# Reads of partial sums moved behind the next stage's remainders, and seven block products for eight in the last quarter of an MLP

## The chip, the cores and the metric

The kernel runs on one core of one Trainium2 chip. The metric is device time in microseconds (us), the median of several runs; before the change it is 2062.33 us over three runs (2061.94 to 2062.93). One more execution was taken with the hardware profiler.

## The reference

One layer of a hybrid encoder over 256 tokens of width 2048: RMSNorm and two token mixers (chunked retention and gated delta rule) with one output projection, cross-attention into 256 memory tokens, a squared-ReLU MLP with hidden width 8192, and a final RMSNorm. All in float32. The change is in the MLP and in the final norm behind it:

```python
h = rms_norm(x, norm_ffn_g[l])
x = x + jnp.square(jax.nn.relu(h @ w_ff1[l])) @ w_ff2[l]
return rms_norm(x, norm_final_g)
```

## The kernel before

**Products in halves.** Every float32 operand is split into two `fp32r` halves: ACT rounds it (`whi`, line 125 for weights), DVE subtracts the rounded half and keeps the remainder (`wlo`, line 126). A product of two split operands is three matmuls: high by high, high by low, low by high. Weights come in loads of 1 MB into one of three tiles `raw`, issued on the queue of SyncE (SP); each is split in two halves of 1024 columns, into three pairs `whi`/`wlo`, and in the MLP every fourth time into a further pair `whx`/`wlx`. So at most four half stages of weights are split ahead of the matmuls.

**The MLP.** It runs in four quarters `fb` of 2048 hidden features. In each quarter first come eight calls of `blocks`, which make the quarter's hidden activations, transposed (lines 209 and 210), square them (`evac_h`) and split them into `hid`. Then they are multiplied with the quarter's 2048 rows of `w_ff2`, and the sums, scaled per token, are added to `res` (256 tokens by 2048 columns) by `add` (line 1138, a DVE instruction that reads PSUM). There are four blocks of 512 columns, n = 0 to 3, and four groups of 512 hidden features, q = 0 to 3.

**Seven for eight.** In the first three quarters `with_seven` does this second half. The part with q = 0, 1 and n = 0, 1 is seen as a product of two by two blocks (two halves of the tokens, even and odd groups of 128 features, two blocks of columns) and is computed as seven block products for eight, in the manner of Strassen and Winograd. It needs sums and differences of the activations (`token_sums`, called in `evac_h`, result `s_hl`) and of four weight blocks `b11`, `b12`, `b22` and `b21`, which `load_block` reads into the two large tiles `rt` and `tr`. A block is in two halves of 1024 columns. The stages, in the order of the matmuls, are `plain(n, q)` (24 matmuls of 128 x 512) and `product` (12 matmuls):

1. plain(3,0)  2. plain(3,1)  3. product of b11 into `shared`  4. plain(3,2)  5. product of b12-b11 into `p5`  6. plain(0,2)  7. product of b22 into own[1][0]  8. plain(3,3)  9. product of b22-b11 into `shared`, where b11 now holds the earlier difference  10. plain(0,3)  11. product of b21  12. plain(2,0)  13. product of b22-b12 into `shared`  14. plain(1,2)  15. plain(2,1)  16. product of b21-b11  17. plain(2,2)  18. plain(2,3)  19. plain(1,3).

`form` splits a block for a product: for stages 5, 9, 13 and 16 it first makes the difference in place on DVE (line 1188), half by half, then rounds (1190) and takes the remainder (1191). `triple` (line 1168) issues the matmuls, each held behind the last matmul of the stage before. After stages 3, 5, 8, 9, 11, 13, 16, 18 and 19 stand the `add` calls that read the finished sums.

**The last quarter** does the second half with `chunk` for each n (lines 166 to 168): 96 matmuls of 128 x 512 per block of columns. `evac_o` adds the sums, takes the sum of squares on ACT (`square_sum`, line 283) and multiplies with the final gain (1274). The last chunk is split more finely, holds the weights of q = 2, 3 in the tiles of the finished activations (`hold`), and its `evac_last` does the final norm and the stores. The gain is loaded into `b11` (`gfin`, line 1267) while the quarter's hidden activations are made.

**Order.** A planner writes each engine's order ahead of the run, from its own estimates of time. Instructions under `high_priority` come earlier when they are ready: fetches, roundings and remainders have offset 100000, `add` has 50000. `issue_after(x)` puts the instructions in it behind x on the same engine. On the chip every engine goes through its order as written.

Of the kernel before, what the change touches and what calls it, by code (L numbers as in the profile page):

```python
# [52 lines left out]
def trunk(ctx: ExitStack, tc: tile.TileContext, x_f, mem_f, positions, lead_f, small_f, w_in, ret_gn_g, w_out, w_xq,  # L53
# [1075 lines left out]
    ssq4 = cp.tile([P, NT, 5], F32, name="ssq4")  # L1129
    s_hl = tuple(fp.tile([P, 4, 512], F32R, name="s" + e, tag="s" + e, bufs=1) for e in "hl")  # L1130
    b11, b12, b22, b21 = (a[:, c:c + 8, :].rearrange("p k s -> p (k s)") for a in (rt, tr) for c in (0, 8))
    gfin = b11
    spare.append(fp)

    def add(n, t, ps, c0=0, c1=512):
        got = res[:, t, n * 512 + c0:n * 512 + c1]
        with tc.high_priority(offset=50000):
            vec.scalar_tensor_tensor(got, ps, rstd3q[:, t:t + 1], got, op0=ALU.mult, op1=ALU.add)
        return got

    def token_sums(i, hs):

# [8 lines left out]
    def with_seven(hid, rows):  # L1151
# [5 lines left out]
        opened, ends = set(), []  # L1157

        def load_block(to, which, n):

            src = rows[0:D // 2, n * 512:(n + 1) * 512].rearrange("(i two p) n -> p i two n", two=2, p=P)[:, :, which, :]
            with tc.issue_after(fetched[-1]), tc.high_priority(offset=100000):
                fetched.append(nc.sync.dma_start(to.rearrange("p (i n) -> p i n", i=4), src).ins)

        def triple(o, lhs, rhs, key, last=False):
            for j, (l, r) in enumerate(((0, 0), (0, 1), (1, 0))):
                with tc.issue_after(ends[-1]) if ends else ExitStack():
                    ins = pe.matmul(o, lhs[l], rhs[r], start=key not in opened, stop=last and j == 2,  # L1168
                                    skip_group_check=True).ins
                opened.add(key)  # L1170
            return ins

        def plain(n, q):
            halves = fetch(cols(rows, n * 512)(q), 4, 512)
            for i in range(4):
                for t in range(NT):
                    ins = triple(own[n][t], [a[:, i, t * P:(t + 1) * P] for a in hid[q]],
                                 [a[:, i % 2, :] for a in halves[i // 2]], (n, t), q == 3 and i == 3)
            ends.append(ins)

        def form(raw, minus=None):
            got = []
            with tc.high_priority(offset=100000):
                for c in range(2):
                    cs = slice(c * 1024, (c + 1) * 1024)
                    if minus:
                        with tc.issue_after(latest["lo"]):
                            vec.tensor_sub(raw[:, cs], *(a[:, cs] for a in minus))
                    hi, lo = (h[:, :1024] for h in half_tiles())
                    latest["hi"] = act.activation(hi, raw[:, cs], AF.Copy).ins  # L1190
                    latest["lo"] = vec.tensor_sub(lo, raw[:, cs], hi.bitcast(F32)).ins
                    got.append((hi.rearrange("p (k n) -> p k n", n=512), lo.rearrange("p (k n) -> p k n", n=512)))
            return got

        def product(o, lhs, halves, key):
# [10 lines left out]
        plain(3, 0)  # L1206
        load_block(b11, 0, 0)
        plain(3, 1)
# [9 lines left out]
        product(own[1][0], summed(3), form(b22), (1, 0))  # L1218
        plain(3, 3)
        load_block(b21, 1, 0)  # L1220
        for t in range(NT):
            add(3, t, own[3][t])
        product(shared, summed(1), form(b11, (b22, b11)), "shared")
        add(1, 0, shared)
        plain(0, 3)
        product(own[0][0], part(1, 0), form(b21), (0, 0))
        add(0, 0, own[0][0])
        plain(2, 0)
        product(shared, summed(2), form(b12, (b22, b12)), "shared")
        add(0, 1, shared)  # L1230
        add(1, 1, shared)
        plain(1, 2)
        plain(2, 1)
        product(own[0][1], part(1, 1), form(b11, (b21, b11)), (0, 1))
        add(0, 1, own[0][1])
        plain(2, 2)
        plain(2, 3)
        for t in range(NT):
            add(2, t, own[2][t])
        plain(1, 3)  # L1240
        for t in range(NT):
            add(1, t, own[1][t])

    for fb in range(4):
        hid = []
        rows = w_ff2[0, fb * D:(fb + 1) * D, :]
        for b2 in range(8):
            hs = fp.tile([P, 2, S], F32, name="hs", tag="hs", bufs=2)
            if b2 % 2 == 0:
                hid.append(quad_a())  # L1250

            def evac_h(b, ps):
                vec.scalar_tensor_tensor(hs[:, b, :], ps, 0.0, ps, op0=ALU.max, op1=ALU.mult)
                qh, ql = (a[:, b2 % 2 * 2 + b, :] for a in hid[-1])
                act.activation(qh, hs[:, b, :], AF.Copy)
                vec.tensor_sub(ql, hs[:, b, :], qh.bitcast(F32))
                if fb < 3 and b2 < 4 and b:
                    token_sums(b2, hs)

            blocks(h3, w_ff1[0], fb * D + b2 * 256, 2, evac_h)  # L1260
            if fb == 0:
                place(b2)
        if fb < 3:
            with_seven(hid, rows)
            continue
        with tc.issue_after(fetched[-1]):
            nc.sync.dma_start(gfin, norm_final_g.partition_broadcast(P))
        for n in range(4):
            ns = slice(n * 512, (n + 1) * 512)

            def evac_o(t, ps, c0, c1):
                got = add(n, t, ps)
                square_sum(ssq4[:, t, n:n + 1], got)
                vec.tensor_mul(got, got, gfin[:, ns])

            def evac_last(t, ps, c0, c1):
                got = add(n, t, ps, c0, c1)
                acc = ssq4[:, t, 4 if c0 else 3:5 if c0 else 4]
                if t == 0:
                    square_sum(acc, got)  # L1280
                else:
                    junk = sm.tile([P, 512], F32, name="junk", tag="junk", bufs=1)
                    vec.scalar_tensor_tensor(junk[:, :256], got, 1.0, got, op0=ALU.mult, op1=ALU.mult, accum_out=acc)
                if not c0:
                    s = sm.tile([P, 1], F32, name="s4", tag="s4")
                    vec.tensor_reduce(s, ssq4[:, t, 0:4], axis=AX.X, op=ALU.add)
                    vec.tensor_scalar(s, s, 1.0 / D, EPS, op0=ALU.mult, op1=ALU.add)
                    sums.append(s)
                else:
                    vec.scalar_tensor_tensor(sums[t], acc, 1.0 / D, sums[t], op0=ALU.mult, op1=ALU.add)  # L1290
                if c1 < 512:
                    return
                r = sm.tile([P, 1], F32, name="r4", tag="r4")
                rsqrt(r, sums[t])
                if t == 0:
                    vec.tensor_mul(res[:, t, ns], res[:, t, ns], gfin[:, ns])
                for c in (0, 3, 1, 2):
                    cs = slice(c * 512, (c + 1) * 512)
# [12 lines left out]


_INS = ["positions", "w_in", "ret_gn_g", "w_out", "w_xq", "w_xkv", "w_xo", "w_ff1", "w_ff2", "norm_final_g"]
# [39 lines left out]
```

## Time and profile before

| | us |
|---|---|
| median of three runs | 2062.33 |
| profiled execution | 2061.57 |
| its span, first to last instruction | 2059.9 |
| PE busy | 2047.6 |
| DVE busy | 1487.2 |
| ACT busy | 1119.7 |
| second halves of the first three quarters | 85.46, 85.79, 85.41 |
| first three blocks of columns, last quarter | 65.31 |

The granted TensorE clock is 0.999 of full speed over the span. PE is matmul, PEld the weight load of a matmul (which overlaps it), DVE VectorE, ACT ScalarE, SP the queue that issues most loads. A group of instructions is given as line, engine, operation, output<-inputs, shapes, count | busy us, mean ns | idle time of the engine just before, with what ended it. A row of a timeline is start, length, engine, line, operation, tiles, count and, in brackets, idle time before it with its releaser. The chain is the work that ended last, followed back from the last instruction.

### The profile page before, as it was taken

How to read it: one execution, taken by the hardware profiler on the slowest of the kernel's cores; microseconds unless marked ns; L12 is line 12 of the kernel's file. 1: busy time of each engine (PE TensorE's matmuls, PEld its weight loads, DVE VectorE, ACT ScalarE, POOL GpSimd, SP SyncE). 2: the span in 40 equal slices, each digit the busy share in tenths (PEclk: the TensorE clock that was granted, in tenths of full speed). 3: DMA queues.
4: the chain of work that ended last, by engine and by line, in shares of the span. 5: the costliest groups of instructions: out<-in, count | busy, mean ns of one | idle time of the engine just before them, and what ended most of it. 6: DMA issues, size and time to landing. Idle time of an engine off the chain costs nothing.

```text
span 2059.9 us, 28433 instructions
## 1 busy us (share of the span) xinstructions
PE 2047.6 (99%) x10886; PEld 1761.5 (86%) x10886; DVE 1487.2 (72%) x2369; ACT 1119.7 (54%) x1817; POOL 36.4 (2%) x50
## 2 busy tenths in 40 slices
PE   9999999999999999999999999999999999999998
PEld 7888888988888888888888898888888888888887
DVE  5887788779667975888567665777777777686654
ACT  5665764575457454755455555555445445444443
POOL 0000000000000000000000000000000000000000
PEclk9999999999999999999999999999999999999999
DMA  9679556455555555555467654679556646746653
GB/s 326 204 248 308 182 186 200 152 195 195 176 177 185 191 182 173 180 189 177 170 214 241 187 184 144 195 173 292 169 179 196 227 163 187 262 134 193 205 197 130
DMA packets 329225, 405.24 MB, mean 197 GB/s; under 512 B 34928, under 2 KB 239360, under 8 KB 328960
## 3 DMA queue, kind: packets, MB, share of 16 engines
q1 hardware_dynamic: 328656, 402.74, 61.0%
q8 instruction: 85, 1.39, 0.3%
q10 hardware_dynamic: 432, 0.69, 0.1%
q14 instruction: 52, 0.43, 0.1%
HBM read 389.74 MB, written 11.55 MB: 195 GB/s over the span
## 4 chain that ended last, share of the span: by engine, by line
PE 98%; DVE 1%; issue 0%; ACT 0%; DMA 0%; SPq 0%; POOLq 0%; POOL 0%; ACTq 0%
PE s L209 34%; PE s L210 18%; PE s L167 9%; PE s L166 9%; PE s L168 9%; PE b L1168 7%; PE s L1168 4%; PE s L398 1%; PE s L400 1%; PE s L399 1%; PE b L793 1%; PE b L696 1%; PE b L826 1%; PE b L138 0%; PE b L137 0%; PE b L139 0%
## 5 line engine op out<-in xcount | busy, mean ns | idle before, releaser
L126 DVE TENSOR_TENSOR wlo<-raw,whi 128x1024 fp32r<-128x1024 f32 x613 | 748.8, 1222 | 354.6 <-ACT whi L125 348.1
L209 PE MATMUL s<-q,whi 128*128 128x512 f32 x2816 | 974.1, 391 | 0.8 <-DVE bo L218 0.6
L125 ACT ACTIVATE whi<-raw 128x1024 fp32r<-128x1024 f32 x613 | 649.2, 1060 | 556.8 <-PE s L209 211.3
L210 PE MATMUL s<-q,wlo 128*128 128x256 f32 x2816 | 771.7, 281 | 0.0
L209 PEld LDWEIGHTS s<-q,whi 128*128 128x128 f32 x2816 | 521.1, 188 | 104.3 <-DVE bo L218 0.9
L210 PEld LDWEIGHTS s<-q,wlo 128*128 128x128 f32 x2816 | 528.7, 188 | 11.1 <-DVE wlo L126 0.8
L167 PE MATMUL s<-wlo,q 128*128 128x512 f32 x788 | 309.7, 393 | 0.0
L168 PE MATMUL s<-whi,q 128*128 128x512 f32 x788 | 307.3, 390 | 0.0
L166 PE MATMUL s<-whi,q 128*128 128x512 f32 x788 | 286.7, 390 | 0.0
L166 PEld LDWEIGHTS s<-whi,q 128*128 128x128 f32 x788 | 147.8, 188 | 30.9
L168 PEld LDWEIGHTS s<-whi,q 128*128 128x128 f32 x788 | 148.1, 188 | 29.7
L167 PEld LDWEIGHTS s<-wlo,q 128*128 128x128 f32 x788 | 148.1, 188 | 29.5
L217 ACT ACTIVATE bo<-s 128x256 f32<-128x256 f32 x192 | 72.9, 380 | 107.4 <-PE s L210 107.3
L218 DVE TENSOR_TENSOR bo<-bo,s 128x256 f32<-128x256 f32 x192 | 80.0, 417 | 53.6 <-ACT bo L217 53.3
L126 DVE TENSOR_TENSOR wlx<-raw,whx 128x1024 fp32r<-128x1024 f32 x59 | 72.2, 1223 | 37.2 <-ACT whx L125 36.3
L1168 PE MATMUL b<-whi,q 128*128 128x512 f32 x300 | 95.7, 389 | 0.0
L209 PE MATMUL s<-q,whx 128*128 128x512 f32 x256 | 89.7, 390 | 0.0
L125 ACT ACTIVATE whx<-raw 128x1024 fp32r<-128x1024 f32 x59 | 62.4, 1058 | 49.5 <-PE s L209 23.0
L210 PE MATMUL s<-q,wlx 128*128 128x256 f32 x256 | 71.3, 280 | 0.0
L655 DVE SCALAR_TENSOR_TENSOR acc<-bo,small,acc 128x255 f32<-128x255 f32 (+1 forms) x144 | 65.2, 479 | 1.8 <-ACT acc L652 0.6
L1168 PEld LDWEIGHTS b<-whi,q 128*128 128x128 f32 x300 | 56.3, 188 | 11.8
L1168 PE MATMUL b<-wlo,q 128*128 128x512 f32 x150 | 58.4, 389 | 0.0
(383 smaller groups left out, 2083.1 us busy)
## 6 DMA issues: line engine op xcount, KB each, us to landing
raw<-w_in SPq DMA_DIRECT2D x143, 1024.0 KB
raw<-w_ff SPq DMA_DIRECT2D x116, 1024.0 KB
raw<-w_xkv SPq DMA_DIRECT2D x29, 1024.0 KB
raw<-w_out SPq DMA_DIRECT2D x16, 1024.0 KB
raw<-w_xq SPq DMA_DIRECT2D x16, 1024.0 KB
raw<-w_xo SPq DMA_DIRECT2D x16, 1024.0 KB
rt<-w_ff SPq DMA_DIRECT2D x6, 1024.0 KB
tr<-w_ff SPq DMA_DIRECT2D x6, 1024.0 KB
```

The costliest lines, as they stand in the source:

```text
L125: latest["hi"] = act.activation(hi[:, cs], src[:, cs], AF.Copy).ins
L126: latest["lo"] = vec.tensor_sub(lo[:, cs], src[:, cs], hi[:, cs].bitcast(F32)).ins
L166: pe.matmul(o, xh, wh, start=first, stop=False)
L167: pe.matmul(o, xh, wl, start=False, stop=False)
L168: pe.matmul(o, xl, wh, start=False, stop=last)
L209: pe.matmul(ps[b], lh, xhl, start=kk == 0, stop=False)
L210: pe.matmul(ps[b][:, :S], ll, xh, start=False, stop=kk == KT - 1)
L217: act.activation(o, ps[b][:, S:], AF.Copy)
L218: vec.tensor_add(o, o, ps[b][:, :S])
L398: pe.matmul(o, xh, wh, start=kk == 0 and c0 == 0, stop=False)
L655: vec.scalar_tensor_tensor(acc[:, d:], ps[:, :S - d], cw[:, j, blk:blk + 1], acc[:, d:], op0=ALU.mult, op1=ALU.add)
L1168: ins = pe.matmul(o, lhs[l], rhs[r], start=key not in opened, stop=last and j == 2, skip_group_check=True).ins
```

## The change

- `add_later` puts an `add` behind the last remainder that has been written when it is called. `read` collects the sums to be read; `read_now` issues them, in the next stage, after that stage's roundings and remainders.
- `form` is gone. `product` splits its block and then, if told so (`then`), makes the difference that a later stage needs: b12-b11 at the end of stage 3, b22-b11 at that of 5, b22-b12 at that of 7, b21-b11 at that of 9.
- plain(1,2) comes before the product of b22-b12 (stages 13 and 14 change places).
- The last quarter uses `with_seven` too, with `last`: block of columns 2 takes the place of 3 in the interleaving, its four plain stages come in the places of plain(3,0) to plain(3,3), and the four plain stages of block 2 further on are left out. Block 3 remains as the finely split last chunk. `token_sums` runs in the last quarter as well.
- The final gain goes into `b22`, and its load stands behind the last fetch of `with_seven`. The square sums and the multiplications with the gain for blocks 0 to 2 come after `with_seven`, the multiplications behind the last `add`.

```diff
-    gfin = b11
+    gfin = b22
...
-            vec.scalar_tensor_tensor(got, ps, rstd3q[:, t:t + 1], got, op0=ALU.mult, op1=ALU.add)
+            latest["add"] = vec.scalar_tensor_tensor(got, ps, rstd3q[:, t:t + 1], got, op0=ALU.mult, op1=ALU.add).ins
         return got
+
+    def add_later(n, t, ps):
+
+        with tc.issue_after(latest["lo"]):
+            add(n, t, ps)
...
+        def read(*those):
+
+            reads.extend(those)
+
+        def read_now():
+            for those in reads:
+                add_later(*those)
+            reads.clear()
...
         def plain(n, q):
             halves = fetch(cols(rows, n * 512)(q), 4, 512)
+            read_now()
...
-        def form(raw, minus=None):
-            got = []
+        def product(o, lhs, raw, key, then=None):
+
+            halves = []
             with tc.high_priority(offset=100000):
-                for c in range(2):
-                    cs = slice(c * 1024, (c + 1) * 1024)
-                    if minus:
-                        with tc.issue_after(latest["lo"]):
-                            vec.tensor_sub(raw[:, cs], *(a[:, cs] for a in minus))
+                for c in range(0, 2048, 1024):
                     hi, lo = (h[:, :1024] for h in half_tiles())
-                    latest["hi"] = act.activation(hi, raw[:, cs], AF.Copy).ins
-                    latest["lo"] = vec.tensor_sub(lo, raw[:, cs], hi.bitcast(F32)).ins
...
+                    latest["hi"] = act.activation(hi, raw[:, c:c + 1024], AF.Copy).ins
+                    latest["lo"] = vec.tensor_sub(lo, raw[:, c:c + 1024], hi.bitcast(F32)).ins
+                    halves.append([a.rearrange("p (k n) -> p k n", n=512) for a in (hi, lo)])
+                for c in range(0, 2048, 1024) if then else ():
+                    with tc.issue_after(latest["lo"]):
+                        vec.tensor_sub(*(a[:, c:c + 1024] for a in then))
+            read_now()
...
+        first = 2 if last else 3
+        plain(first, 0)
         load_block(b11, 0, 0)
+        plain(first, 1)
         load_block(b12, 0, 1)
-        product(shared, part(0, 0), form(b11), "shared")
-        add(0, 0, shared)
-        plain(3, 2)
+        product(shared, part(0, 0), b11, "shared", (b11, b12, b11))
+        read((0, 0, shared))
+        plain(first, 2)
         load_block(b22, 1, 1)
-        product(p5, summed(0), form(b11, (b12, b11)), "p5")
-        add(1, 0, p5)
-        add(1, 1, p5)
+        product(p5, summed(0), b11, "p5", (b11, b22, b11))
+        read((1, 0, p5), (1, 1, p5))
         plain(0, 2)
...
+        product(own[1][0], summed(3), b22, (1, 0), (b12, b22, b12))
+        plain(first, 3)
         load_block(b21, 1, 0)
+        read(*((first, t, own[first][t]) for t in range(NT)))
+        product(shared, summed(1), b11, "shared", (b11, b21, b11))
+        read((1, 0, shared))
         plain(0, 3)
...
+        product(own[0][0], part(1, 0), b21, (0, 0))
+        read((0, 0, own[0][0]))
+        if not last:
+            plain(2, 0)
         plain(1, 2)
...
+        product(shared, summed(2), b12, "shared")
+        read((0, 1, shared), (1, 1, shared))
+        if not last:
+            plain(2, 1)
+        product(own[0][1], part(1, 1), b11, (0, 1))
+        read((0, 1, own[0][1]))
+        if not last:
+            plain(2, 2)
+            plain(2, 3)
+            read(*((2, t, own[2][t]) for t in range(NT)))
         plain(1, 3)
+        read(*((1, t, own[1][t]) for t in range(NT)))
+        for those in reads:
+            add(*those)
...
-                if fb < 3 and b2 < 4 and b:
+                if b2 < 4 and b:
                     token_sums(b2, hs)
...
+        with_seven(hid, rows, fb == 3)
         if fb < 3:
-            with_seven(hid, rows)
             continue
         with tc.issue_after(fetched[-1]):
             nc.sync.dma_start(gfin, norm_final_g.partition_broadcast(P))
-        for n in range(4):
+        for t in range(NT):
+            for n in range(3):
+                ns = slice(n * 512, (n + 1) * 512)
+                got = res[:, t, ns]
+                square_sum(ssq4[:, t, n:n + 1], got)
+                with tc.issue_after(latest["add"]):
+                    vec.tensor_mul(got, got, gfin[:, ns])
+        for n in range(3, 4):
             ns = slice(n * 512, (n + 1) * 512)
-
-            def evac_o(t, ps, c0, c1):
-                got = add(n, t, ps)
-                square_sum(ssq4[:, t, n:n + 1], got)
-                vec.tensor_mul(got, got, gfin[:, ns])
...
-            last = n == 3
             sums = []
-            chunk(hid, cols(rows, n * 512), evac_last if last else evac_o, hold=quad_b if last else None)
+            chunk(hid, cols(rows, n * 512), evac_last, hold=quad_b)
```

More of the change, by code (lines that the diff above doesn't have):

```diff
@@ L1149, in token_sums, with with_seven @@
         split([a[:, i, :] for a in s_hl], sv.rearrange("p a s -> p (a s)"))
-    def with_seven(hid, rows):
+    def with_seven(hid, rows, last):
         own = [stream_ps() for _ in range(2)]
@@ L1156, in with_seven @@
         own += [[bank(), bank()]] * 2
-        opened, ends = set(), []
+        opened, ends, reads = set(), [], []
         def load_block(to, which, n):
@@ L1179, in plain @@
             ends.append(ins)
-        def form(raw, minus=None):
-            got = []
+        def product(o, lhs, raw, key, then=None):
+            halves = []
             with tc.high_priority(offset=100000):
-                for c in range(2):
-                    cs = slice(c * 1024, (c + 1) * 1024)
-                    if minus:
-                        with tc.issue_after(latest["lo"]):
-                            vec.tensor_sub(raw[:, cs], *(a[:, cs] for a in minus))
-                    hi, lo = (h[:, :1024] for h in half_tiles())
[L1190 to L1195, printed above, removed]
+                for c in range(0, 2048, 1024):
+                    hi, lo = (h[:, :1024] for h in half_tiles())
+                    latest["hi"] = act.activation(hi, raw[:, c:c + 1024], AF.Copy).ins
[5 more added lines that the diff above has]
+            read_now()
             for i in range(4):
@@ L1204, in summed @@
             return lambda i: [a[:, i, j * P:(j + 1) * P] for a in s_hl]
-        plain(3, 0)
+        first = 2 if last else 3
+        plain(first, 0)
         load_block(b11, 0, 0)
-        plain(3, 1)
+        plain(first, 1)
         load_block(b12, 0, 1)
-        product(shared, part(0, 0), form(b11), "shared")
-        add(0, 0, shared)
-        plain(3, 2)
+        product(shared, part(0, 0), b11, "shared", (b11, b12, b11))
+        read((0, 0, shared))
+        plain(first, 2)
         load_block(b22, 1, 1)
-        product(p5, summed(0), form(b11, (b12, b11)), "p5")
@@ L1215, in with_seven @@
-        add(1, 0, p5)
-        add(1, 1, p5)
+        product(p5, summed(0), b11, "p5", (b11, b22, b11))
+        read((1, 0, p5), (1, 1, p5))
         plain(0, 2)
-        product(own[1][0], summed(3), form(b22), (1, 0))
-        plain(3, 3)
+        product(own[1][0], summed(3), b22, (1, 0), (b12, b22, b12))
+        plain(first, 3)
         load_block(b21, 1, 0)
-        for t in range(NT):
-            add(3, t, own[3][t])
-        product(shared, summed(1), form(b11, (b22, b11)), "shared")
@@ L1224, in with_seven @@
-        add(1, 0, shared)
+        read(*((first, t, own[first][t]) for t in range(NT)))
+        product(shared, summed(1), b11, "shared", (b11, b21, b11))
+        read((1, 0, shared))
         plain(0, 3)
[L1226 to L1231, printed above, removed]
-        plain(1, 2)
-        plain(2, 1)
-        product(own[0][1], part(1, 1), form(b11, (b21, b11)), (0, 1))
@@ L1235, in with_seven @@
[L1235 to L1239, printed above, removed]
+        product(own[0][0], part(1, 0), b21, (0, 0))
+        read((0, 0, own[0][0]))
+        if not last:
+            plain(2, 0)
+        plain(1, 2)
+        product(shared, summed(2), b12, "shared")
[4 more added lines that the diff above has]
+        read((0, 1, own[0][1]))
@@ L1240, in with_seven @@
+        if not last:
+            plain(2, 2)
+            plain(2, 3)
+            read(*((2, t, own[2][t]) for t in range(NT)))
         plain(1, 3)
-        for t in range(NT):
-            add(1, t, own[1][t])
+        read(*((1, t, own[1][t]) for t in range(NT)))
+        for those in reads:
+            add(*those)
     for fb in range(4):
```

## The prediction

> **What bounds the kernel now.** I read the page first (busy shares, then the chain that ended last), then the chain inside each quarter of the MLP, then the busy time by stretch, then the timelines of DVE, ACT and SP around the places where the chain leaves PE.
>
> ```profile
> PE 2047.6 (99%) x10886; PEld 1761.5 (86%) x10886; DVE 1487.2 (72%) x2369; ACT 1119.7 (54%) x1817; POOL 36.4 (2%) x50
> PE 98%; DVE 1%; issue 0%; ACT 0%; DMA 0%; SPq 0%; POOLq 0%; POOL 0%; ACTq 0%
> ```
>
> PE carries 98% of the chain, so only two things can shorten the time: fewer matmuls, or PE not waiting. The change touches the four second halves of the MLP alone. The chain there, in order of time (start us, us, what, count), first quarter, then the second and the third from their starts, their stalls and their ends:
>
> ```profile
> 1443.23 21.97 PE b L1168 x96
> 1465.20 8.18 PE s L1168 x36
> 1473.38 4.78 PE b L1168 x21
> ...
> 1478.18 0.79 DVE res L1138 x2
> ...
> 1479.53 1.23 DVE wlo L1191
> ...
> 1480.80 1.45 PE b L1168 x5
> ...
> 1498.74 5.46 PE s L1168 x24
> 1504.20 5.44 PE b L1168 x24
> ...
> 1523.24 5.45 PE s L1168 x24
> ...
> 1616.87 21.86 PE b L1168 x96
> ...
> 1652.39 1.19 DVE res L1138 x2
> ...
> 1653.63 1.23 DVE wlx L1191
> ...
> 1697.21 5.45 PE s L1168 x24
> ...
> 1790.84 21.94 PE b L1168 x96
> ...
> 1870.81 5.45 PE s L1168 x24
> ```
>
> A run of 24 matmuls without a wait takes 5.44 us: 226.7 ns each. A quarter has 12 plain stages of 24 and 7 products of 12, 372 matmuls, 84.33 us at that pace. The chain gives 1528.69 - 1443.23 = 85.46, 1702.66 - 1616.87 = 85.79 and 1876.26 - 1790.84 = 85.42: excesses of 1.13, 1.46 and 1.09 us, 3.68 in all. Some 0.1 of each is the 0.01 to 0.04 us by which a stage that changes banks is longer (5.46 and 5.45 for 5.44); the rest, about 3.38, is PE waiting for a remainder `wlo` in a product that forms its difference in place. DVE at that place, and what ACT waited for:
>
> ```profile
> 1475.36 1.23 DVE L1191 TENSOR_TENSOR wlo<-rt,whi 128x1024 fp32r<-128x1024 f32 x1 [1.21 <-ACT whi L1190]
> 1476.50 1.22 DVE L1188 TENSOR_TENSOR rt<-tr,rt 128x1024 f32<-128x1024 f32 x1
> 1478.18 1.43 DVE L1138 SCALAR_TENSOR_TENSOR res<-b,rstd3q,res 128x512 f32<-128x512 f32 x2 [0.46 <-PE b L1168]
> 1479.53 1.22 DVE L1191 TENSOR_TENSOR wlo<-rt,whi 128x1024 fp32r<-128x1024 f32 x1
> ...
> 1477.84 1.06 ACT L1190 ACTIVATE whi<-rt 128x1024 fp32r<-128x1024 f32 x1 [2.51 <-DVE rt L1188]
> ```
>
> The difference (1.22), its rounding (1.06) and its remainder (1.23) form one chain per half block, the next half's difference is behind the remainder, and two sums that wait 0.46 us for PE stand before the last remainder. That is stage 9; stages 5 and 13 lose 0.1 to 0.2 in the same way.
>
> **The change, part by part.**
>
> ```profile
> 1443.07:1528.53 85.46, 85.07 (x375) 69.59 (x373) 64.64 (x65) 40.12 (x42) 0.00 (x0) 1.00 0.51 168
> ...
> 1964.27:2029.58 65.31, 65.31 (x291) 54.06 (x289) 41.40 (x43) 32.98 (x40) 0.00 (x0) 1.00 0.59 201
> ...
> 1702.50:1790.68 88.18, 88.18 (x514) 78.16 (x512) 61.59 (x96) 44.34 (x65) 0.00 (x0) 1.00 0.72 228
> 1876.09:1964.27 88.18, 88.18 (x513) 78.16 (x512) 55.61 (x76) 42.25 (x61) 0.00 (x0) 1.00 0.67 205
> ```
>
> (Busy time by stretch: length, then PE, weight loads, DVE, ACT and POOL with counts, clock, DMA share, GB/s.)
>
> *Last quarter in seven products.* The first three blocks of columns are 288 matmuls before (65.31 us, 226.8 each, nothing idle) and 8 x 24 + 7 x 12 = 276 after: 12 x 226.7 ns = 2.72 us less. About six more bank changes give back 0.1: net 2.62. The Trainium skill (TensorE: Matmul & The Clock Gate, Back-to-back issue gap) states about 131 ns per matmul of 512 columns in a stream with weight loads; by that the 12 would save 1.57 us and the total would be 4.95. The trace has 226.7, so it disagrees with the page.
>
> *Token sums in the last quarter.* Four calls more. The two stretches of the hidden layer above are one with them and one without: DVE 61.59 against 55.61, ACT 44.34 against 42.25, PE 88.18 both times. They cost nothing; DVE's 27 us of idle time hide them, and without that cover they would cost 6.
>
> *Differences made earlier.* The eight half differences of a quarter stay, and move from the head of stages 5, 9, 13 and 16 to the tail of 3, 5, 7 and 9. The chain of 1.22 + 1.06 + 1.23 loses its first link, and no rounding waits 2.51 us for DVE any more. The price is DVE's room in stages 3 to 11, by the groups of the first quarter:
>
> ```profile
> L126 DVE TENSOR_TENSOR wlo<-raw,whi 128x1024 fp32r<-128x1024 f32 x15 | 18.3, 1224 | 7.9 <-ACT whi L125 7.8
> ...
> L1188 DVE TENSOR_TENSOR rt<-tr,rt 128x1024 f32<-128x1024 f32 x6 | 7.3, 1219 | 0.0
> ...
> L1138 DVE SCALAR_TENSOR_TENSOR res<-b,rstd3q,res 128x512 f32<-128x512 f32 x10 | 7.1, 746 | 0.5 <-PE b L1168 0.5
> ...
> 1452.59 1.23 DVE L126 TENSOR_TENSOR wlo<-raw,whi 128x1024 fp32r<-128x1024 f32 x1 [1.48 <-ACT whi L125]
> ...
> 1467.20 2.35 DVE L1191 TENSOR_TENSOR wlo<-tr,whi 128x1024 fp32r<-128x1024 f32 x2
> ...
> 1445.98 0.50 SPq L1163 DMA_DIRECT2D tr<-w_ff  x1
> ```
>
> These stages are 156 matmuls, 35.4 us of PE. DVE needs 18 remainders, 8 differences and 6 sums: 26 x 1.22 + 6 x 0.75 = 36.2 us when each is counted whole, 26 x 1.13 + 6 x 0.68 = 33.5 when they follow one another (two remainders take 2.35). So DVE is nearly full there, but it enters with a lead: the remainder at 1452.59 is for stage 4, which starts after 60 matmuls, 13.6 us behind 1443.07, at 1456.7. A lead of 4.1 us against a lack of 0.8 at worst: I take zero. Each difference needs its second block landed; the last of the four loads of a quarter is issued at 1445.98, in stage 1, and first used in stage 9, so I count no wait.
>
> *Sums behind the next stage's remainders.* 13 sums of 0.75 us per quarter stay. Each still waits for PE, and now the remainders of the stage after next stand behind it. Split tiles are four half stages deep, so the second of those remainders could not be made before PE ends the same stage anyway. Behind that event stand at most 2 sums (1.41), 2 differences (2.35) and that remainder (1.23), 5.0 us, while PE has a product and half a plain stage, 5.44, before it needs it. Margin 0.4: zero. So the 3.38 us go; what is late next is nothing in the first three quarters.
>
> *Final gain and square sums.* The 1 MB load moves from the hidden layer to behind the last fetch of the products, ahead of the last four weight fetches on SP; six square sums and six multiplications go behind the last sum.
>
> ```profile
> 1939.62 0.58 SPq L1267 DMA_DIRECT2D rt<-norm_final_g  x1
> ...
> 2010.37 11.25 SPq L113 DMA_DIRECT2D raw<-w_ff  x4
> ...
> 2015.29 2.01 ACT L125 ACTIVATE q<-raw 128x1024 fp32r<-128x1024 f32 x2 [0.77 <-DMA raw<-w_ff]
> ...
> 2020.86 2.01 ACT L125 ACTIVATE q<-raw 128x1024 fp32r<-128x1024 f32 x2 [0.89 <-DMA raw<-w_ff]
> 2023.94 1.06 ACT L125 ACTIVATE whi<-raw 128x1024 fp32r<-128x1024 f32 x1 [1.07 <-DMA raw<-w_ff]
> ...
> 2030.75 0.61 ACT L283 ACTIVATE junk<-res 128x512 f32<-128x512 f32 x1
> ...
> 2032.02 1.29 DVE L1274 TENSOR_TENSOR res<-res,rt 128x512 f32<-128x512 f32 x2
> 2046.49 0.75 DVE L1138 SCALAR_TENSOR_TENSOR res<-s,rstd3q,res 128x512 f32<-128x512 f32 x1 [13.18 <-PE s L168]
> ```
>
> DVE idles 13.18 us before the tail: 6 x 0.65 (1.29 for two) = 3.9 us of multiplications fit, and so do six square sums of 0.61 with a short read-out each on ACT, whose last one before the tail is as early; uncovered these would cost 4 to 5 at the end. SP waits 0.58 longer. A weight fetch reaches its rounding 4.9 us after its issue (2010.37 to 2015.29). Stages 14, 16 and the difference products read no `raw`, so the last fetches can go out earlier; I take zero, with 1.3 to 4.4 as the other end (rival B).
>
> **Sum.** -2.62 - 3.38 = -6.0 us. The profiled execution takes 2061.57 (span 2059.9), 0.76 below the median of the three runs, 2062.33. So 2055.6 on its own scale, and 2056.3 as a median.
>
> **Rivals.** A change of 0.2%, 4.1 us, is about what a measurement of this kernel can tell from none.
>
> *B: the last chunk starts late.* Its first weights may find a `raw` tile only when the last plain stage is split: tile free 2.72 us before that stage starts, rounding and remainder 2.28, landing 4.9, rounding and remainder 2.28, so ready 6.74 into a stage of 5.44: PE waits 1.3, and up to 3.1 more if the gain's 1 MB is in front (the nearest two of these loads are 3.1 apart, 2020.86 and 2023.94). Gain 1.6 to 4.7, about 2059.2. For it: the roundings of these fetches already wait for DMA. Against it: three tiles, and fewer stages that use them.
>
> *C: the wait moves.* The order on DVE is written out ahead of the run. Where a waiting sum or a difference falls before a remainder that PE needs, the 3.38 us come back elsewhere: 2062.33 - 2.62 = 2059.7. For it: the second quarter, the same program, lost 0.3 more than the others. The Trainium skill says that DVE's queue is strictly first in, first out (TensorE: Matmul & The Clock Gate, Architectural detail); the 0.46 us at 1478.18 with a remainder behind it agrees.
>
> *D: DVE becomes the bound in stages 3 to 11; slower.* Place: the differences in front of the remainders. Without the lead (4.1) the lack is 0.8, and if the six sums wait 0.46 each as at 1478.18, 2.8 more: 3.6 us a quarter, 14.4 in four, 8.4 net of the gain: 2070.7. It decides from a lack of (6.0 + 4.1) / 4 = 2.5 us a quarter beyond the lead. Against it: 64.64 of 85.46 us busy, and that lead.
>
> **How the numbers follow.** Forecast 0.64 (its own range 2054.9 to 2057.7), B 0.17, C 0.11, D 0.08. Below 2058.2 lie nearly all of the forecast and a third of B: faster 0.69; same 0.22 (the rest of B, C, a little of D); slower 0.09. The range runs from all 3.68 and 2.72 gone on the profiled scale with 0.3 of scatter, 2054.9, to C's end, 2060.0; outside lie D and some 0.05 more.
>
> **What would show it.** Right: in the chain no DVE or ACT piece within the first three quarters; each 84.4 us long; the three blocks of the last quarter 62.7 us; hidden layer 88.18; no `whi` waiting 2.51 us for `rt`. Wrong: a `wlo` before a PE piece in stages 4 to 11 (C, D); a `whi` waiting for DMA with PE idle as the last block of columns starts (B); a square sum or multiplication after the last matmul.

## The result and the profile after

The changed kernel takes 2056.73 us (median of ten runs, 2054.98 to 2058.18); the kernel before, run ten times beside it, 2062.25 (2059.84 to 2062.93). The ratio is 0.9974, with a 95% interval of 0.9964 to 0.9984: 5.5 us less. The forecast was 2056.3. The profiled execution after takes 2056.91 (span 2055.2), before 2061.57 (span 2059.9): 4.66 less.

The first part of the page after the change, and its row on the chain by engine:

```profile
PE 2043.9 (99%) x10874; PEld 1759.8 (86%) x10874; DVE 1511.4 (74%) x2409; ACT 1130.3 (55%) x1827; POOL 36.4 (2%) x50
...
PE 96%; DVE 1%; DMA 1%; issue 1%; ACT 1%; SPq 0%; POOLq 0%; POOL 0%; DVEq 0%; ACTq 0%
```

Twelve matmuls fewer, and PE still carries the chain; DMA and ACT have a per cent of it that they had not before. The chain after, in order of time (start us, us, what, count): the first quarter, start and end of the second and the third, then the last quarter up to its last stage.

```profile
1443.80 21.79 PE b L1182 x96
...
1473.74 8.16 PE b L1182 x36
1481.90 8.16 PE s L1182 x36
...
1522.70 5.45 PE s L1182 x24
...
1616.33 21.79 PE b L1182 x96
...
1695.24 5.45 PE s L1182 x24
...
1788.87 21.79 PE b L1182 x96
...
1867.77 5.45 PE s L1182 x24
...
1961.40 21.78 PE b L1182 x96
...
1998.43 1.14 DVE wlo L126
...
1999.59 4.95 DMA raw<-w_ff
...
2004.56 1.07 ACT q L125
...
2005.65 2.37 DVE q L126 x2
...
2008.04 4.97 DMA raw<-w_ff
...
2013.03 1.07 ACT q L125
...
2016.40 1.22 DVE wlo L1203
2017.62 0.33 DVE res L1138
...
2018.20 0.74 DVE res L1138
2018.94 1.14 DVE wlo L126
...
2020.13 5.30 PE s L1182 x22
```

The three quarters are 1528.15 - 1443.80 = 84.35, 1700.68 - 1616.33 = 84.35 and 1873.22 - 1788.87 = 84.35 us, against 85.46, 85.79 and 85.42: 3.62 gone, and no piece of DVE or ACT is left in them. In the last quarter the chain leaves PE. It runs through two loads of `raw`, the roundings and remainders `q` of the held weights of the last column block, a remainder `wlo` of the last product, two sums `res` and a remainder `wlo` of the last plain stage (plain(1,3)), and comes back to PE only at 2020.13.

The busy time by stretch shows what that costs (length, then PE, weight loads, DVE, ACT and POOL with counts, clock, DMA share, GB/s): the first quarter, the hidden layer after it, and the last quarter from its first matmul to the end of its last.

```profile
1443.63:1527.99 84.36, 84.36 (x374) 69.83 (x373) 64.72 (x65) 41.38 (x42) 0.00 (x0) 1.00 0.52 176
1527.99:1616.17 88.18, 88.18 (x514) 78.16 (x512) 61.57 (x96) 44.34 (x65) 0.00 (x0) 1.00 0.71 228
...
1961.23:2047.54 86.31, 85.82 (x422) 72.15 (x420) 66.34 (x76) 44.62 (x57) 0.55 (x1) 1.00 0.38 133
```

The same stretch of the kernel before:

```profile
1964.27:2052.20 87.93, 87.93 (x434) 74.47 (x432) 47.74 (x56) 38.66 (x51) 0.55 (x1) 1.00 0.45 154
```

The last quarter gains 87.93 - 86.31 = 1.62 us, where 12 matmuls are worth 2.72. Together with the quarters' 3.62 (3.60 by stretches of 85.46, 85.79 or 85.80, and 85.42 against 84.36) that is 5.2. The profiled runs differ by 4.66 because the first quarter starts 0.56 later after the change (1443.63 against 1443.07), in a part that the change leaves alone.

What stands in front of the last product's remainder, ACT and then DVE after the change (start, length, engine, line, operation, tiles, count, idle time before with its releaser):

```profile
2004.56 2.01 ACT L125 ACTIVATE q<-raw 128x1024 fp32r<-128x1024 f32 x2 [1.24 <-DMA raw<-w_ff]
...
2013.03 2.01 ACT L125 ACTIVATE q<-raw 128x1024 fp32r<-128x1024 f32 x2 [1.49 <-DMA raw<-w_ff]
2014.95 1.05 ACT L1202 ACTIVATE whi<-rt 128x1024 fp32r<-128x1024 f32 x1
```

```profile
2014.13 2.36 DVE L126 TENSOR_TENSOR q<-raw,q 128x1024 fp32r<-128x1024 f32 x2 [0.92 <-ACT q L125]
2016.40 1.22 DVE L1203 TENSOR_TENSOR wlo<-rt,whi 128x1024 fp32r<-128x1024 f32 x1
```

The held weights `q` are used last, but ACT and DVE make them first, and wait 1.24 and 1.49 us for their loads. Only then comes the rounding `whi` for the product that PE is about to start. Its remainder, begun at 2016.40, ends at 2017.62, and PE's matmul at 2017.68 is 0.43 us late. Another, at 2020.13, is 0.38 late, and the matmul behind each of them 0.11: 1.03 us in all. (The expectations below have 0.27 for 0.38; the matmul before 2020.13 has 256 columns, and those follow one another after 0.12 us here, not 0.23.)

### The profile page after: what moved, and what is told of

Its sections match the earlier page's. It is cut to its first block, busy times and chain, and to the rows that moved or that the text cites. A ratio compares the mean times of both kernels' runs of the same rounds, so it can differ in the third digit from the quotient of the medians.

```text
span 2055.2 us, 28469 instructions
## 1 busy us (share of the span) xinstructions
PE 2043.9 (99%) x10874; PEld 1759.8 (86%) x10874; DVE 1511.4 (74%) x2409; ACT 1130.3 (55%) x1827; POOL 36.4 (2%) x50
## 4 chain that ended last, share of the span: by engine, by line
PE 96%; DVE 1%; DMA 1%; issue 1%; ACT 1%; SPq 0%; POOLq 0%; POOL 0%; DVEq 0%; ACTq 0%
PE s L209 33%; PE s L210 17%; PE b L1182 9%; PE s L167 8%; PE s L168 8%; PE s L166 8%; PE s L1182 5%; PE s L399 1%; PE s L398 1%; PE s L400 1%; PE b L793 1%; PE b L826 1%; PE b L138 0%; DMA raw<-w_ff 0%; PE b L137 0%
## 5 line engine op out<-in xcount | busy, mean ns | idle before, releaser
L167 PE MATMUL s<-wlo,q 128*128 128x512 f32 x716 | 281.7, 393 | 0.0
L168 PE MATMUL s<-whi,q 128*128 128x512 f32 x716 | 279.4, 390 | 0.0
L166 PE MATMUL s<-whi,q 128*128 128x512 f32 x716 | 258.9, 390 | 0.0
L166 PEld LDWEIGHTS s<-whi,q 128*128 128x128 f32 x716 | 134.3, 188 | 28.0
L168 PEld LDWEIGHTS s<-whi,q 128*128 128x128 f32 x716 | 134.6, 188 | 27.0
L167 PEld LDWEIGHTS s<-wlo,q 128*128 128x128 f32 x716 | 134.6, 188 | 26.7
L1182 PE MATMUL b<-whi,q 128*128 128x512 f32 x360 | 114.7, 389 | 0.0
L126 DVE TENSOR_TENSOR wlx<-raw,whx 128x1024 fp32r<-128x1024 f32 x54 | 66.0, 1222 | 28.1 <-ACT whx L125 27.2
L125 ACT ACTIVATE whx<-raw 128x1024 fp32r<-128x1024 f32 x54 | 57.2, 1060 | 52.5 <-PE s L209 23.0
L1182 PE MATMUL s<-whi,q 128*128 128x512 f32 x248 | 79.8, 389 | 0.0
L1182 PEld LDWEIGHTS b<-whi,q 128*128 128x128 f32 x360 | 67.6, 188 | 14.1
L1182 PE MATMUL b<-wlo,q 128*128 128x512 f32 x180 | 70.1, 389 | 0.0
```

The lines of the kernel that those rows point to most:

```text
L125: latest["hi"] = act.activation(hi[:, cs], src[:, cs], AF.Copy).ins
L126: latest["lo"] = vec.tensor_sub(lo[:, cs], src[:, cs], hi[:, cs].bitcast(F32)).ins
L166: pe.matmul(o, xh, wh, start=first, stop=False)
L167: pe.matmul(o, xh, wl, start=False, stop=False)
L168: pe.matmul(o, xl, wh, start=False, stop=last)
```

## The experiments

My theory: the three quarters lost nothing but waits, which go because the differences are made early; the 12 matmuls are worth 226.7 ns each; and about 1 us of that is lost to the held weights that stand ahead on ACT and DVE. The rivals are B (the last block starts late because of landing tiles or the gain's 1 MB), C (the wait moves) and D (DVE is near its limit). All stretches in this table are read from the traces: the three quarters, and the last quarter to the end of its last matmul. Each ratio is to runs of the kernel before taken beside that kernel (medians of 2062.25 to 2062.51). The diffs are against the changed kernel and shortened: in the kernels that ran, constants choose between the variants.

| kernel | median us | ratio to before, 95% | quarters us | last us |
|---|---|---|---|---|
| before | 2062.25 | 1 | 85.46, 85.80, 85.42 | 87.93 |
| after | 2056.73 | 0.9974 (0.9964 to 0.9984) | 84.36 x3 | 86.31 |
| first three alone | 2058.78 | 0.9982 (0.9973 to 0.9991) | 84.36 x3 | 87.93 |
| last alone | 2061.35 | 0.9994 (0.9985 to 1.0003) | 85.38, 85.81, 85.44 | 86.61 |
| sums behind, no early differences | 2061.91 | 0.9998 (0.9988 to 1.0007) | 85.66, 84.58, 85.67 | 87.93 |
| early differences, sums at once | 2058.40 | 0.9981 (0.9972 to 0.9991) | 84.36 x3 | 87.93 |
| differences made three times | 2066.82 | 1.0020 (1.0011 to 1.0030) | 87.53, 86.40, 87.76 | 87.93 |
| differences made twice | 2058.65 | 0.9982 (0.9973 to 0.9991) | 84.36 x3 | 87.93 |
| after, a pair of split tiles less | 2068.02 | 1.0027 (1.0016 to 1.0038) | 86.65, 86.73, 86.66 | 90.63 |
| after, gain behind the last block | 2057.74 | 0.9978 (0.9969 to 0.9987) | 84.36 x3 | 86.60 |
| after, held weights late | 2056.03 | 0.9970 (0.9959 to 0.9982) | 84.36 x3 | 85.18 |
| after, once more | 2056.95 | 0.9976 (0.9966 to 0.9986) | 84.37, 84.35, 84.36 | 86.34 |
| held weights late, once more | 2056.32 | 0.9970 (0.9960 to 0.9981) | 84.36 x3 | 85.18 |

**The two places apart.** The first three quarters alone, with the last quarter as before:

```diff
-                if b2 < 4 and b:
+                if fb < 3 and b2 < 4 and b:
...
-        with_seven(hid, rows, fb == 3)
         if fb < 3:
+            with_seven(hid, rows, False)
             continue
...
-        for n in range(3, 4):
+        for n in range(4):
```

> The first three quarters with their differences made early and their sums behind the remainders; the last quarter in 8 products as before. My theory (the waits in the first three quarters were the whole excess, and all of it goes; the changed kernel's three quarters are 84.36, 84.35 and 84.36 us for 85.46, 85.79 and 85.41): each quarter 84.4, 3.65 us less in all, so 0.9982 of the time before, some 2058.6. Rival C (the wait moves, only the 12 matmuls count): quarters of 85.4 again, ratio 1.000. Rival that the last quarter's change pays for part of it: the same 3.65 here, but then the last quarter alone gains more than its own.

And the last quarter alone, with the first three in the manner and order of before:

```diff
+        early = later = last
...
+                    if first and not early:
+                        with tc.issue_after(latest["lo"]):
+                            vec.tensor_sub(*(a[:, c:c + 1024] for a in first))
                     hi, lo = (h[:, :1024] for h in half_tiles())
```

> The last quarter as in the changed kernel (7 products, everything early), the first three as before. My theory: quarters of 85.4 to 85.8 as before; the last quarter saves 12 matmuls (2.72 us at 226.7 ns) and gives 0.9 back where the last column block's held weights stand ahead of the others on ACT and DVE, so 1.7 to 1.8 us less: 0.9992 of the time before, some 2060.5. At 131 ns a matmul the 12 would be 1.57 and, with the 0.9 given back, the gain 0.7. If the 0.9 comes only from the earlier quarters running ahead (the DMA queues nearer), it is absent here and the gain is 2.7.

The quarters alone are 84.36 three times and the time is 0.9982 of before, 3.7 us less: my theory, to 0.1. The last quarter alone leaves the others at 85.4 to 85.8 and gains 87.93 - 86.61 = 1.32 by the trace, for 1.7 to 1.8 expected; the times alone do not show this gain, since their interval reaches over 1. The pauses are there without any earlier quarter running ahead, somewhat longer; its stretch and chain in the last quarter:

```profile
1964.13:2050.74 86.61, 85.84 (x422) 72.15 (x420) 66.35 (x76) 44.60 (x57) 0.55 (x1) 1.00 0.38 133
```

```profile
2002.49 5.17 DMA raw<-w_ff
...
2011.17 5.04 DMA raw<-w_ff
```

The loads took 5.17 and 5.04 here for 4.95 and 4.97, and the stretch is 0.30 longer. Two kernels from further down fit in: 4.95 and 5.04 with a stretch of 86.34 (after, once more), 5.14 and 5.04 with 86.60 (gain behind). What is lost here follows the duration of these loads.

**Differences or sums.** Two kernels, both with the last quarter as before. In the first the sums go behind the next stage's remainders, but the differences stay in front of their product, and plain(1,2) comes behind the product of b22-b12, as before:

```diff
-        product(p5, summed(0), b11, "p5", (b11, b22, b11))
+        product(p5, summed(0), b11, "p5", first=(b11, b12, b11))
```

(and so for the other three). In the second the differences are early and the sums at once:

```diff
         def read(*those):
 
-            reads.extend(those)
+            for one in those:
+                add(*one)
```

> First three quarters: the sums go behind the next stage's remainders as in the changed kernel, but each difference is made in the product that needs it, ahead of its rounding, as before; last quarter as before. Theory of the prediction (the chain difference, rounding, remainder of 1.22 + 1.06 + 1.23 us is what PE waits for): most of the 1.1 to 1.5 us of each quarter stays, quarters of 85.2 to 85.5. Theory that it is the two sums that stand, waiting 0.46 for PE, before the last remainder: the long pause of stage 9 (0.55, 1.1 and 0.55) goes, the ones of 0.1 to 0.2 in stages 5, 9 and 13 stay, quarters of 84.6 to 84.8. Walking DVE's order along with the durations of the profile gives the second.

> First three quarters: the differences are made stages ahead as in the changed kernel, but the sums are read as soon as their matmuls are done, as before; last quarter as before. Theory of the prediction (the difference's place in the chain): all pauses go, quarters of 84.36 as with both. Theory of the sums: the pause of stage 9 (0.55, 1.1, 0.55) stays at least in half, quarters of 84.7 or more. Walking DVE's order along with the durations of the profile gives no pause.

With the sums alone the quarters are 85.66, 84.58 and 85.67: the second gains 1.22, the others lose 0.2 each. The pause has moved from stage 9 to stage 10. Chain of its first quarter there, and DVE:

```profile
1479.21 1.40 DVE res L1143 x2
1480.62 1.14 DVE wlo L128
...
1481.80 7.99 PE s L1194 x34
```

```profile
1478.07 1.23 DVE L1219 TENSOR_TENSOR wlo<-rt,whi 128x1024 fp32r<-128x1024 f32 x1 [1.21 <-ACT whi L1218]
1479.21 1.40 DVE L1143 SCALAR_TENSOR_TENSOR res<-b,rstd3q,res 128x512 f32<-128x512 f32 x2
1480.53 1.22 DVE L128 TENSOR_TENSOR wlo<-raw,whi 128x1024 fp32r<-128x1024 f32 x1
```

DVE still idles 1.21 us for the rounding of the difference that it made itself. The sums no longer stand before this product's remainder; they stand before the next plain stage's, and PE waits for that one. That is rival C, in a kernel in which half the change is left out. With early differences alone all pauses are gone, as with both. This second kernel is no test of the sums, though: with the differences early, DVE and ACT go through the same instructions in the same order in these quarters' traces, whether the sums are held back or not (the second kernel beside the first three quarters alone). So in the first three quarters the whole 3.6 us come without holding the sums back. The kernels with early differences also have stages 13 and 14 in their new order, which was not tried apart; what could hang on that is the pause of stage 13, 0.07 to 0.15 us a quarter (the chain before has 8.31, 8.23 and 8.31 us there for 36 matmuls that take 8.16). I had expected the sums to take most of the pause by themselves; in two of three quarters they took none.

**How far DVE is from its limit.** With the last quarter as before, the first half of each difference is made several times:

```diff
                 for c in range(0, 2048, 1024) if then else ():
                     with tc.issue_after(latest["lo"]):
-                        vec.tensor_sub(*(a[:, c:c + 1024] for a in then))
+                        for _ in range(1 if c else 3):
+                            vec.tensor_sub(*(a[:, c:c + 1024] for a in then))
```

> First three quarters as in the changed kernel but the first half of each difference is made three times over (the same value again, up to rounding): 8 operations of 1.13 us more a quarter, 9.0 us of DVE in stages 3 to 9; last quarter as before. This loads the place of rival D. By the prediction's sum (lack 0.8 when each operation is counted whole, lead 4.1) PE loses 0.8 + 9.0 - 4.1 = 5.7 us a quarter, 17 in three; counted as they follow one another (lack of -1.9) 3.0 a quarter, 9 in three. Walking DVE's order along, with the lead of the split tiles filled again at each product, gives 0.2 to 0.8 a quarter, 1 to 2 in three: then DVE was further from being the bound than the prediction had it. If DVE were the bound already, all 9.0 a quarter would show.

The chain of the first quarter in that kernel:

```profile
1470.44 3.41 DVE rt L1224 x3
...
1479.43 2.36 DVE rt L1224 x2
...
1486.52 1.15 DVE wlx L128
...
1487.71 5.28 PE s L1194 x22
```

PE loses 3.17, 2.04 and 3.40 us. My walk along DVE's order (0.2 to 0.8) was wrong; the prediction's own count of operations that follow one another (3.0) was right. Taken as a difference, 9.0 us more meet 5.6 to 7.0 us of room, for which the prediction's rows give 4.1 of lead and 1.9 of slack, 6.0. With two for three:

> As the kernel that makes the first half of each difference three times, but twice: 4 operations of 1.13 us more a quarter, 4.5 us of DVE in stages 3 to 9. Three times over (9.0 us) cost 3.17, 2.04 and 3.40 us a quarter, so DVE had 5.6 to 7.0 us to spare there, about the 4.1 of lead and 1.9 of room that the prediction's rows give (6.0). If that is one stock that any stage can draw on, 4.5 us cost nothing: quarters of 84.4, 2058.6. If the pauses are local (each repeated operation in front of the next stage's remainder costs its own time wherever it stands), half of the cost stays: quarters of 85.4 to 86, some 2063.

(Made twice, the subtraction undoes itself, so this kernel multiplies the undone half block; the instructions are those of a real difference.) The chain's start and end of its first quarter:

```profile
1444.86 21.79 PE b L1194 x96
...
1523.76 5.45 PE s L1194 x24
```

1529.21 - 1444.86 = 84.35: 4.5 us of extra DVE work cost nothing. So the lead acts as one stock, of which the change leaves at least 4.5 us. D's mechanism is real, and it starts between 4.5 and 9.0 us of DVE work a quarter beyond what the change asks.

**Where the lead is kept.** The changed kernel with three pairs of split tiles in the MLP for four:

```diff
-    spare.append(fp)
```

> The changed kernel with three pairs of split half tiles in the MLP for four. The prediction's margin of 0.4 us for a sum behind the remainders rests on a product and half a plain stage (5.44 us) between the release of a tile and its use; with a pair less a half stage of 1.36 (product) or 2.72 (plain) is gone. Theory: PE then waits about 0.4 at four stages of a quarter, 1.5 us a quarter, 6 in all, so some 2063; quarters of 85.9. Rival: DVE's lead carries it whatever the depth, quarters of 84.4 and 2056.7.

Each quarter loses 2.3 us, and the last one 4.3: more than the 1.5 expected. ACT and then DVE in its first quarter, from stage 8 on:

```profile
1477.92 1.06 ACT L1218 ACTIVATE whi<-rt 128x1024 fp32r<-128x1024 f32 x1 [1.88 <-PE b L1194]
```

```profile
1480.15 1.22 DVE L1224 TENSOR_TENSOR rt<-tr,rt 128x1024 f32<-128x1024 f32 x1
1481.29 0.75 DVE L1143 SCALAR_TENSOR_TENSOR res<-b,rstd3q,res 128x512 f32<-128x512 f32 x1
1481.95 1.22 DVE L1224 TENSOR_TENSOR rt<-tr,rt 128x1024 f32<-128x1024 f32 x1
1483.08 0.75 DVE L1143 SCALAR_TENSOR_TENSOR res<-b,rstd3q,res 128x512 f32<-128x512 f32 x1
1483.74 2.35 DVE L128 TENSOR_TENSOR wlo<-raw,whi 128x1024 fp32r<-128x1024 f32 x2
```

ACT waits 1.88 us for PE to free a pair, DVE stands behind it, and then two differences and two sums are in front of the remainder that PE needs: its matmul at 1485.02 starts 1.40 us late. The differences that cost nothing in the changed kernel stand in PE's way here, so it is the fourth pair that hides them; it was in the kernel before too. What three pairs cost without early differences was not run, so their share of the 2.3 us is open.

**What PE waits for ahead of the last block.** The 1 MB of the gain behind the last block's four fetches; `before` is a function handed to `chunk` that holds the load, the square sums and the multiplications, and it is called behind the loop over q = 0, 1:

```diff
-        with tc.issue_after(fetched[-1]):
-            nc.sync.dma_start(gfin, norm_final_g.partition_broadcast(P))
...
+        if before and hold:
+            before(2)
```

> The changed kernel, with the 1 MB load of the final gain issued behind the last column block's four fetches and no longer ahead of them (its square sums and multiplications move with it). My theory (the gain's load ends 8 us before the held weights can be fetched at all, since those wait for a landing tile): the first of the four fetches starts at the same 28.4 us after the third block's start as in the changed kernel, the pauses of 0.54 and 0.38 stay, the time is that of the changed kernel, 2056.7. Rival B as I wrote it (the gain's 1 MB in front delays the last block): the pauses shrink by more than half, some 0.5 to 0.9 us less. If the multiplications now come too late, up to 4 us more at the end.

The held weights (q = 2, 3) fetched behind the loop over q = 0, 1, not ahead of it:

```diff
-        held = {q: fetch(pieces_of(q), 4, 512, hold=hold) for q in ((2, 3) if hold else ())}
+        held = {}
...
+        if hold:
+            held = {q: fetch(pieces_of(q), 4, 512, hold=hold) for q in (2, 3)}
         for part in parts:
```

> The changed kernel, with the held weights of the last column block (row blocks 2 and 3, used last) fetched and rounded behind those of row blocks 0 and 1 and no longer ahead of them. My theory: the two PE pauses before the last block (0.43 + 0.11 at 2017.68 and 0.27 + 0.11 at 2020.13) come from ACT and DVE standing at the held weights' roundings, which wait 1.24 and 1.49 us for their DMA; without them in front PE has no pause of over 0.05 there, 0.9 us less than the changed kernel, about 2055.9. If the pauses come from DMA itself being late (three landing tiles for the weights, the 1 MB of the gain), the first fetch of the last block is as late as the held one was and the 0.9 us stay, or grow.

With the gain behind, the stretch is 86.60, and the second pair of held roundings waits for its load as in the changed kernel (1.49 there):

```profile
1960.22:2046.82 86.60, 85.83 (x422) 72.15 (x420) 66.35 (x76) 44.59 (x57) 0.55 (x1) 1.00 0.38 133
```

```profile
2012.29 2.01 ACT L127 ACTIVATE q<-raw 128x1024 fp32r<-128x1024 f32 x2 [1.59 <-DMA raw<-w_ff]
```

So the gain's load is not the cause. With the held weights late, the stretch is 85.18 and ACT at the last plain stage and at the held weights shows:

```profile
1960.87:2046.05 85.18, 85.17 (x422) 72.15 (x420) 66.82 (x76) 45.16 (x57) 0.55 (x1) 1.00 0.39 135
```

```profile
2014.18 1.06 ACT L127 ACTIVATE whi<-raw 128x1024 fp32r<-128x1024 f32 x1 [0.29 <-PE b L1194]
...
2024.04 2.01 ACT L127 ACTIVATE q<-raw 128x1024 fp32r<-128x1024 f32 x2 [2.05 <-DMA raw<-w_ff]
```

ACT waits 2.05 us for the same loads, but behind the roundings that PE needs first, and PE is busy for 85.17 of the 85.18 us. The fetch and the rounding moved together here; which of the two would do alone was not tried. Both kernels once more on one chip, to see whether the pauses were a chance of one execution:

> The changed kernel once more, beside the one with the held weights late, on one chip. My theory: quarters of 84.36 three times, the last one 86.3 us from its first matmul to the last matmul's end, 0.9 of it in the two pauses before the last column block; 2056.7. If the pauses were a chance of that one execution, they are absent here.

> The changed kernel with the held weights of the last column block fetched and rounded behind the others, once more. My theory: no pause over 0.05 us before the last block, 85.2 us from the last quarter's first matmul to the last matmul's end, 1.1 us less than the changed kernel, so some 2055.6 to 2056.0: less than both, by 0.05% against the changed kernel, which the times alone cannot tell apart.

The stretches come back as 86.34 and 85.18. The version with the held weights late is the fastest here: 1.13 and 1.16 us less than the changed kernel by the traces. The medians, 0.9970 (0.9960 to 0.9981) and 0.9976 (0.9966 to 0.9986) of before, agree with that but could not show it alone.

## Why the prediction was right, step by step

- **Last quarter, 12 matmuls: -2.62 forecast, -2.75 measured** where nothing delays them (87.93 - 85.18), 229 ns each. By the Trainium skill's 131 ns (TensorE: Matmul & The Clock Gate, Back-to-back issue gap) the estimate would have been 1.57; the runs disagree with it here as the row of 226.7 did. The 0.1 set aside for more bank changes was wrong: 36 matmuls with changes between them take 8.16, 226.7 each.
- **Waits in the quarters: -3.38 forecast, -3.60 measured.** The mechanism was right and the term too small: I left 0.1 in each quarter for bank changes, from stages of 5.45 and 5.46. A quarter after the change is 84.36, and 372 x 226.7 is 84.33, so all but 0.03 was waiting.
- **Which edit does it.** The step on the differences is right: without them in the chain the pause goes. The step on the sums is right in its zero and wrong in its working: I gave a margin of 0.4 us for a new place in the order, but with early differences DVE's order is no other than without this edit.
- **Token sums, 0:** the hidden layer is 88.17 to 88.18 in each quarter, the last one with them included. **DVE's lead, 0:** quarters without a pause, and room for 4.5 us more.
- **Final gain and square sums, 0:** from the last matmul's end to the end of the span it is 7.66 before (2059.86 - 2052.20) and 7.65 after (2055.19 - 2047.54).
- **The last fetches, 0 with 1.3 to 4.4 as other end: this step failed.** It costs 1.13, near the size of B's lower end, and not by B's way. B looked for the block's first weights late in a landing tile, with the gain in front. The tile does matter, since the held load goes out only at 1999.59, but it is late for weights that are used last; PE stops because their roundings stand ahead of others on ACT and DVE, and it stops in the last product and the last plain stage, ahead of that block. So the three blocks took 64.03 us (1961.40 to 2025.43, with two matmuls of the last block among them) for 62.7. The prediction read the order of the fetches on SP and not what the same order does to the roundings. The Trainium skill's strict first in, first out for DVE (TensorE: Matmul & The Clock Gate, Architectural detail), which it had beside rival C, is the rule that bears on this: the trace agrees, with `wlo` at 2016.40 behind `q<-raw,q`. The held weights stood first in the kernel before too, where their roundings waited 0.77 and 0.89 us for loads and PE had no pause. What differs is the work behind them: two products follow each other in the last quarter now, so that four split half stages last 4 x 1.36 = 5.4 us of PE and not 4 x 2.72 = 10.9, and DVE has 66.34 us to do in this stretch for 47.74. Which of these lets the wait through was not tried.

So by the traces -3.60 - 2.75 + 1.13 = -5.2, for -6.0 forecast and -5.5 by the medians. Two terms that were 0.2 and 0.1 too small took up a third of the one that was missed, and the medians lie 0.3 nearer to the forecast than the stretches do: both are luck.

## What to carry to other kernels

Price an operation in an in-order queue by what it may have to wait for, not by its duration, and price it again when the work behind it changes: a rounding that waits for a load stops everything written behind it, whoever needs it. Data used last should be fetched and prepared last, even where its storage is free early. And before crediting an edit that reorders work, see whether the written order differs at all.

## What was not expected

A stretch without waits repeats to 0.02 us from run to run (84.35 to 84.37 for each of the three quarters in eight executions), while the time at which the first quarter starts does not. Its first chain row in the kernel with the sums alone, and in the one with early differences alone, after the same work up to there:

```profile
1442.42 21.95 PE b L1194 x96
```

```profile
1445.11 21.79 PE b L1194 x96
```

They lie 2.7 us apart. In the two traces of the changed kernel this start differs by 0.87 us (1443.80 and 1444.67) and the span by 0.9; in the two with the held weights late by 0.29 and 0.3. So what scatters in these traces lies ahead of the MLP, and a gain of 1 us in the MLP can be read from a stretch of the trace and not from the run's time. Where in the earlier part it arises was not tried.
